# A three-branch decoder layer: the convolution's product turned token-major, the state space started eight weight pieces later, and vector and scalar work placed anew

## The chip, the cores and the metric

The kernel runs on one core of a Trainium2 chip. The metric is the time of one execution on the device in microseconds (us); before the change it is 1209.36 us, the median of three runs (1208.78 to 1209.36). The core has a matrix engine (TensorE, PE in the profile), a vector engine (VectorE, DVE), a scalar engine (ScalarE, ACT), GpSimd (POOL) and a queue for transfers (SyncE, SP). Each works through its own list of instructions in order and waits for the others by semaphores.

## The reference

One decoder layer on 256 tokens of width 2048, all in float32. One wide input projection feeds three branches; each branch is projected back to 2048 columns, weighted by a sigmoid gate and summed; an output projection, a residual and a norm follow.

```python
h = rms_norm(x, norm_w); proj = h @ w_in            # 18464 columns, split up
o_sb  = stick_breaking_attention(sb_q, sb_k, sb_v) * silu(sb_z)
xbc   = silu(causal_depthwise_conv(ssd_xbc, conv_w, conv_b))      # 4096 channels, 4 taps
x_ssm, b_in, c_in = split(xbc)
dt = softplus(ssd_dt + dt_bias);  a = -exp(a_log)
y  = ssd_chunked_scan(x_ssm heads, dt, a, b_in, c_in) + d_skip * x_ssm
o_ssd = gated_group_rms_norm(y, ssd_z, ssd_norm_w)
o_mem = memory_cross_attention(mem_q, rms_norm(mem), w_mem_kv) * silu(mem_z)
g_sb, g_ssd, g_mem = split(sigmoid(gate_pre + b_gate))
merged = g_sb*(o_sb @ w_branch_sb) + g_ssd*(o_ssd @ w_branch_ssd) + g_mem*(o_mem @ w_branch_mem)
out = rms_norm(x + merged @ w_out, final_norm_w)
```

In the scan a head's 256x256 matrix of decays is `exp(a_cum[l] - a_cum[s])` below the diagonal, times `cb[l,s]`; it multiplies `x * dt`.

## The kernel before

All large products stream their weights from memory in 408 **pieces** of 512 KB. A piece is loaded (`raw`, 4 buffers, L206), split by ScalarE into its upper half `wh` (L146) and by VectorE into the rest `wl = raw - wh` (L150), 3 buffers each, and used by TensorE in three matmuls per tile (upper by upper, upper by rest, rest by upper). So ScalarE and VectorE run ahead of TensorE by as much as three buffers allow: the split of a piece can begin when TensorE is done with the piece three earlier.

There are two forms of the product. `gemm` (L249) takes pieces of 256 rows by 512 columns, has the activations stationary and gives tokens in the partitions: 12 matmuls of 512 columns a piece. `gemm_cols` (L211), used by the convolution alone, takes 512 rows by 256 columns, has the weights stationary and gives channels in the partitions: for each of its 4 row tiles two matmuls of 512 columns (L229) and two of 256 (L233). Where `gemm`'s result is wanted with channels in the partitions, `turning` (L302) does it: two 32x32-block transposes on VectorE, one write to memory and four reads back from ScalarE's queue.

Order is set by hand. The pieces of all products form one sequence. After each piece `pump()` (L185) does two things: it runs what `defer(fn, n)` has put down for n pieces later, and it takes one step of one of two **lanes**, in turn. A lane is a queue of Python generators, and each `yield` ends a step. The attention heads (`sb_head`, L672) are in the lanes during the projections, the state space (`ssd_group`, L815, eight groups of four heads, worked in pairs) afterwards. So an instruction's place on its engine is fixed when the program is built, between the splits of two pieces.

In what follows **c1** is the first piece after the convolution's last, c2 the next, and so on. Pieces c1 to c8 are the first gate product, c9 to c12 the first branch product (`w_branch_mem`), c13 to c20 the next gate, and so on by twelve: four gates and four products of the memory branch, the same of the stick-breaking branch, then the state-space branch, whose products have eight pieces.

The steps of a state-space pair, in order: `cb` (two matmuls on TensorE, and the loads of the running decays `dec`, L823 to L828); `xs = x*dt`, a copy of `cb` to `cbs` and the causal mask (L830 to L846); the exponentials (`decay`, L849, four instructions of 128x128 for each of three tiles) and their product with `cbs` (`weigh`, L856); `y`, the products of both groups of the pair together (L869 to L883, 48 matmuls of 64x128); then skip, gate and norm (L887 to L916). The exponentials need ScalarE's table of exp and ln, the gates' sigmoid (`sigmoid`, L809) another; a change of table is an ACT_TABLE_LOAD of its own. `x` is turned for the products by `turn_x` (L758), once for two groups.

The convolution's four taps (`taps`, L745) are one multiply-add L747 and three L750 on VectorE for each of 32 tiles of 128 channels. `gate_evac` (L941) adds the bias on VectorE (L945) and takes the sigmoid on ScalarE; `branch_evac` (L949) multiplies by the gate (L954, L956) and sums the branches on GpSimd (L957).

Of the kernel before, what the change touches and what calls it, by code (L numbers as in the profile page):

```python
# [10 lines left out]
F32 = mybir.dt.float32  # L11
# [30 lines left out]
def trunk_kernel(  # L42
# [91 lines left out]
    nacx = const.tile([P, SSD_HEADS], F32, name="nacx")  # L134

# [371 lines left out]
    def dt_steps():  # L507
# [54 lines left out]
        nc.vector.tensor_tensor(nacx, nac[:, 0], ps[:, 2], ALU.subtract)  # L562
        yield
        pt = bank([SSD_HEADS, T], "act")
# [173 lines left out]
    def conv_evac(i0):  # L738
        def evac(acc):
            u = tmp.tile([P, 2, T], F32, tag="cu", name=nm("cu"), bufs=2)  # L740
            fold(u, acc)
            for b in range(2):
                defer(lambda b=b: taps(u[:, b], i0 + b), 1 + 2 * b)
# [9 lines left out]
        return evac  # L753

    x_rows = {}
    x_used = []

    def turn_x(m):  # L758

        src = cT[m // 2][:, 4 * (m % 2):4 * (m % 2) + 4]  # L760
        scratch = dram.tile([P, 4, T], F32, name=nm("scratch"))
        blocks = tmp.tile([P, 4, 2, 4, 32], F32, tag="blocks", name=nm("blocks"), bufs=1)
        rows = tmp.tile([P, 4, 2, 4, 32], F32, tag="turned", name=nm("turned"), bufs=1)

        def block(k):
            nc.vector.transpose(blocks[:, :, :, k].rearrange("p j t c -> p t j c"),
                                src[:, k].rearrange("p (t j c) -> p t j c", t=2, c=32))
# [41 lines left out]
    def sigmoid(a):  # L809
        nc.scalar.activation(a, a, AF.Sigmoid)  # L810
        tables[0] = False

    tables = [False]

    def ssd_group(g):  # L815

        heads = range(4 * g, 4 * g + 4)
        xT = [cT[i // 8][:, i % 8] for i in (2 * g, 2 * g + 1)]
# [4 lines left out]
        for j in range(2):  # L823
            nc.sync.dma_start(dec[j], acT[j, h0:h0 + 4].partition_broadcast(P))
# [298 lines left out]
```

## Time and profile before

| | |
|---|---|
| median of three runs | 1209.36 us |
| the profiled execution's own time | 1209.97 us |
| its span, first to last instruction | 1208.2 us |
| TensorE busy | 1197.4 us (99%) |
| VectorE busy | 792.0 us (66%) |
| ScalarE busy | 633.6 us (52%) |
| GpSimd busy | 51.5 us (4%) |
| granted TensorE clock | 0.999 |

The profile is one execution, taken by the hardware profiler. Its page gives each engine's busy time, the chain of work that ended last, and groups of instructions by line; the trace behind it answers for any stretch: a timeline row is start, duration, engine, line, operation, output<-input, count, and in brackets the time that the engine sat idle before it and what ended that. The ends of matmuls are modelled and overlap the next ones, so TensorE's pace is read from the starts. On ScalarE and VectorE too the next instruction may start a little before the one ahead of it ends.

### The profile page before, as it was taken

How to read it: one execution, taken by the hardware profiler on the slowest of the kernel's cores; microseconds unless marked ns; L12 is line 12 of the kernel's file. 1: busy time of each engine (PE TensorE's matmuls, PEld its weight loads, DVE VectorE, ACT ScalarE, POOL GpSimd, SP SyncE). 2: the span in 40 equal slices, each digit the busy share in tenths (PEclk: the TensorE clock that was granted, in tenths of full speed). 3: DMA queues.
4: the chain of work that ended last, by engine and by line, in shares of the span. 5: the costliest groups of instructions: out<-in, count | busy, mean ns of one | idle time of the engine just before them, and what ended most of it. 6: DMA issues, size and time to landing. Idle time of an engine off the chain costs nothing.

```text
span 1208.2 us, 15619 instructions
## 1 busy us (share of the span) xinstructions
PE 1197.4 (99%) x5812; PEld 1004.6 (83%) x5812; DVE 792.0 (66%) x1037; ACT 633.6 (52%) x842; POOL 51.5 (4%) x50
## 2 busy tenths in 40 slices
PE   8999999999999999999999999999999999999997
PEld 7888888888888888888888888888888888888886
DVE  5676664545555555888887858677677755555662
ACT  6754443364454444545665756485757534444551
POOL 0000000000000000010100000000000010110002
PEclk9999999999999999999999999999999999999999
DMA  9978687877775777665668676667756677778962
GB/s 315 363 225 237 205 251 234 251 234 214 205 210 171 216 220 228 190 186 167 187 176 258 212 223 216 214 206 218 223 181 201 209 216 220 227 220 280 295 205 88
DMA packets 170893, 265.72 MB, mean 220 GB/s; under 512 B 12032, under 2 KB 68032, under 8 KB 170688
## 3 DMA queue, kind: packets, MB, share of 16 engines
q1 hardware_dynamic: 134304, 227.41, 61.6%
q10 hardware_dynamic: 36512, 37.31, 9.5%
q8 instruction: 45, 0.74, 0.3%
q14 instruction: 32, 0.26, 0.1%
HBM read 249.97 MB, written 14.71 MB: 219 GB/s over the span
## 4 chain that ended last, share of the span: by engine, by line
PE 97%; issue 1%; DMA 1%; DVE 0%; ACT 0%; SPq 0%; POOLq 0%; POOL 0%; DVEq 0%; ACTq 0%
PE acc L269 25%; PE acc L270 25%; PE acc L271 25%; PE acc L229 10%; PE acc L233 5%; PE acc L458 1%; PE acc L459 1%; PE acc L457 1%; PE y L876 1%; DMA raw<-in_w_mem_kv_dram 1%; PE dtp L519 0%; PE acc L1077 0%; PE acc L1076 0%; PE acc L1075 0%; PE spo L710 0%
## 5 line engine op out<-in xcount | busy, mean ns | idle before, releaser
L150 DVE TENSOR_TENSOR wl<-raw,wh 128x1024 fp32r<-128x1024 f32 (+1 forms) x409 | 504.2, 1235 | 319.3 <-ACT wh L146 315.0
L146 ACT ACTIVATE wh<-raw 128x1024 fp32r<-128x1024 f32 (+1 forms) x409 | 431.5, 1056 | 434.9 <-PE acc L271 340.7
L269 PE MATMUL acc<-wh,hT 128*128 128x512 f32 x896 | 350.9, 392 | 0.0
L271 PE MATMUL acc<-wh,hT 128*128 128x512 f32 x896 | 348.8, 389 | 0.0
L270 PE MATMUL acc<-wl,hT 128*128 128x512 f32 x896 | 348.8, 389 | 0.0
L271 PEld LDWEIGHTS acc<-wh,hT 128*128 128x128 f32 x896 | 168.2, 188 | 35.5
L269 PEld LDWEIGHTS acc<-wh,hT 128*128 128x128 f32 x896 | 168.3, 188 | 34.1 <-issue 0.3
L270 PEld LDWEIGHTS acc<-wl,hT 128*128 128x128 f32 x896 | 168.3, 188 | 33.4
L229 PE MATMUL acc<-hT,wh 128*128 128x512 f32 x512 | 161.6, 397 | 0.0
L233 PEld LDWEIGHTS acc<-hT,wl 128*128 128x128 f32 x512 | 96.2, 188 | 22.7
L233 PE MATMUL acc<-hT,wl 128*128 128x256 f32 x512 | 100.7, 278 | 0.0
L229 PEld LDWEIGHTS acc<-hT,wh 128*128 128x128 f32 x512 | 78.1, 189 | 0.1
L269 PE MATMUL acc<-wh,oD 128*128 128x512 f32 x128 | 49.8, 389 | 0.0
L270 PE MATMUL acc<-wl,oD 128*128 128x512 f32 x128 | 49.8, 389 | 0.0
L271 PE MATMUL acc<-wh,oD 128*128 128x512 f32 x128 | 49.8, 389 | 0.0
L750 DVE SCALAR_TENSOR_TENSOR cT<-cu,wcols,cT 128x255 f32<-128x255 f32 (+2 forms) x96 | 46.4, 483 | 3.4
L957 POOL TENSOR_TENSOR merged<-merged,sig 128x512 f32<-128x512 f32 x16 | 25.8, 1637 | 512.3 <-DVE sig L956 512.3
L269 PE MATMUL acc<-wh,mT 128*128 128x512 f32 x96 | 37.3, 389 | 0.0
L270 PE MATMUL acc<-wl,mT 128*128 128x512 f32 x96 | 37.3, 389 | 0.0
L271 PE MATMUL acc<-wh,mT 128*128 128x512 f32 x96 | 37.3, 389 | 0.0
L270 PEld LDWEIGHTS acc<-wl,oD 128*128 128x128 f32 x128 | 24.0, 188 | 5.0
L271 PEld LDWEIGHTS acc<-wh,oD 128*128 128x128 f32 x128 | 24.0, 188 | 5.0
(239 smaller groups left out, 1283.6 us busy)
## 6 DMA issues: line engine op xcount, KB each, us to landing
raw<-in_w_in_dram SPq DMA_DIRECT2D x288, 512.0 KB, 4.3
raw<-in_w_branch_ssd_dram SPq DMA_DIRECT2D x32, 512.0 KB, 4.5
raw<-in_w_mem_kv_dram SPq DMA_DIRECT2D x31, 512.0 KB, 6.4
scratch<-blocks ACTq DMA_DIRECT2D x24, 512.0 KB, 4.3
raw<-in_w_out_dram SPq DMA_DIRECT2D x24, 512.0 KB, 6.1
turned<-scratch ACTq DMA_DIRECT2D x64, 128.0 KB, 4.6
raw<-in_w_branch_mem_dram SPq DMA_DIRECT2D x16, 512.0 KB, 4.8
raw<-in_w_branch_sb_dram SPq DMA_DIRECT2D x16, 512.0 KB, 5.0
```

The source lines that it names most:

```text
L146: nc.scalar.activation(hi, src, AF.Copy, **({} if scale is None else {"scale": scale}))
L150: nc.vector.tensor_tensor(lo, src, h32, ALU.subtract)
L229: nc.tensor.matmul(halves[b], wh[:, kt - k0, b * P:(b + 1) * P], lhs.both(kt), start=first, stop=False, skip_group_check=True)
L233: nc.tensor.matmul(halves[b][:, 1], wl[:, kt - k0, b * P:(b + 1) * P], lhs.at(kt)[0], start=False, stop=last, skip_group_check=True)
L269: nc.tensor.matmul(a, lh[:, tt], wh[:, j], start=first, stop=False)
L270: nc.tensor.matmul(a, lh[:, tt], wl[:, j], start=False, stop=False)
L271: nc.tensor.matmul(a, ll[:, tt], wh[:, j], start=False, stop=last)
L457: nc.tensor.matmul(a, lh[:, tt], wh[:, g], start=first, stop=False)
L458: nc.tensor.matmul(a, lh[:, tt], wl[:, g], start=False, stop=False)
L459: nc.tensor.matmul(a, ll[:, tt], wh[:, g], start=False, stop=last)
L750: nc.vector.scalar_tensor_tensor(a[:, s:T], u[:, 0:T - s], convw[:, 3 - s, i:i + 1], a[:, s:T], ALU.mult, ALU.add)
L957: nc.gpsimd.tensor_tensor(merged[t][:, cs], merged[t][:, cs], sig[:, t], ALU.add)
```

## The change

1. The convolution's product uses `gemm` and `turning` in place of `gemm_cols`. Out of the turned tile ScalarE copies two 128x512 tiles, and the first tap becomes a ScalarE activation with scale and bias.
2. The state space starts at c12, not c4: its `cb` matmuls stand after c12 and c13, not c4 and c5. For the state-space branch two gates are computed ahead of its first product, not one, so `finish()` is eight pieces later too.
3. `xs` loses its factor dt; the exponentials take `ln dt` in their bias instead (`shift`, from a new Ln in `dt_steps`), and `xs` is a plain copy on ScalarE, two pieces ahead of `y`'s step. A third load fills `dec[2]`.
4. The exponentials stand in three steps of four instructions, not two of six, and the first four in the same step as the copy `cbs`. A group's step moves on only when `x_rows` is there.
5. SiLU of two groups of x (the third and the fourth 512 channels) is done late, at the first two gates' sigmoids that follow: two sigmoids of 128x512 on ScalarE, each followed by a product on VectorE (`silu_late`); the buffer `sl` is single.
6. `gate_evac` adds its two halves in two pieces; `branch_evac` spreads its products, and the sum of the branches is on VectorE.

```diff
@@ dt_steps
+        nc.vector.tensor_scalar(z, dts, 1e-37, None, ALU.max)
+        nc.scalar.activation(z, z, AF.Ln)
+        yield
+        nc.vector.tensor_tensor(shift[:, 0:3:2], nac, z, ALU.add)
+        nc.vector.tensor_tensor(shift[:, 1], nacx, z[:, 0], ALU.add)
@@ convolution
+    def conv(i0):
+        when = (1, 3, 11, 13) if i0 == 12 else (1, 3, 5, 7)
+        def use(cols):
+            for k in (0, 2):
+                u = tmp.tile([P, 2, T], F32, tag="cu", name=nm("cu"), bufs=2)
+                nc.scalar.activation(blocked(u), tiles(cols, k, 2), AF.Copy)
+                for b in range(2):
+                    defer(lambda u=u, i=k + b: taps(u[:, i % 2], i0 + i), when[k + b])
...
         def taps(u, i):
             a = cT[i // 8][:, i % 8]
-            nc.vector.tensor_scalar(a, u, convw[:, 3, i:i + 1], convb[:, i:i + 1], ALU.mult,
-                                    ALU.add)
+            nc.scalar.activation(a, u, AF.Identity, scale=convw[:, 3, i:i + 1],
+                                 bias=convb[:, i:i + 1])
...
+        return turning(use)
+    def silu_late():
+        g = waiting.pop(0)
+        for k in range(4 * (g % 2), 4 * (g % 2) + 4, 2):
+            a = cT[g // 2][:, k:k + 2]
+            r = tmp.tile([P, 2, T], F32, tag="sl", name=nm("sl"), bufs=1)
+            nc.scalar.activation(r, a, AF.Sigmoid)
+            nc.vector.tensor_tensor(a, a, r, ALU.mult)
+        silu_done.add(g)
+    def squash(a):
+        nc.scalar.activation(a, a, AF.Sigmoid)
+        if waiting:
+            silu_late()
+        tables[0] = False
-        for j in range(2):
-            gemm_cols(hT, NKT, w_in, C_XBC + g * GW + 2 * j * P, conv_evac(4 * g + 2 * j))
+        gemm(hT, NKT, w_in, C_XBC + g * GW, conv(4 * g))
@@ ssd_group
-        decay(1)
-        decay(0, 0, 2)
-        yield
-        decay(0, 2, 4)
-        decay(2)
-        weigh(1)
-        yield
-        weigh(0)
-        weigh(2)
+        nc.scalar.activation(cbs, cb, AF.Copy)
+        decay(1)
+        for j in (0, 2):
+            nc.vector.tensor_tensor(dec[j], dec[j], over(cmask), ALU.add)
+        yield
+        decay(0)
+        weigh(1)
+        yield
+        decay(2)
+        weigh(0)
+        yield
+        while g // 2 not in x_rows:
+            yield
+        weigh(2)
...
-    defer(start_ssd, 4)
+    defer(lambda: turn_when(0), 7)
+    defer(start_ssd, 12)
@@ gates and branches
         def evac(acc):
-            for t in (1, 0):
-                nc.vector.tensor_tensor(sig[:, t], acc[t], sig[:, 0], ALU.add)
-            defer(lambda: sigmoid(sig), 1)
+            part(acc, 1)
+            defer(lambda: part(acc, 0), 1)
+            defer(lambda: squash(sig), 2)
...
-                    nc.gpsimd.tensor_tensor(merged[t][:, cs], merged[t][:, cs], sig[:, t],
-                                            ALU.add)
+        def add(t):
+            nc.vector.tensor_tensor(merged[t][:, cs], merged[t][:, cs], sig[:, t], ALU.add)
...
+            for gate in ((0, 1), (), (2,), (3,))[g] if br == 2 else (g,):
```

Three places show how it moves instructions. A row is line, operation, output<-input and size; the rows stand as their engine takes them, and each `wh` or `wl` row is the split of one piece.

VectorE, where the first pair's `dec` tiles get their mask. Before (`xs` is x*dt, `turned` the turned x):

```order
L150 TENSOR_TENSOR wl_5704<-raw_5701,wh_5703 128x1024
L835 TENSOR_TENSOR xs_5719<-turned_5255,dts 128x128 x4
L846 TENSOR_TENSOR dec_5665<-dec_5665,cmask 128x512
L846 TENSOR_TENSOR dec_5667<-dec_5666,cmask 128x512
L150 TENSOR_TENSOR wl_5734<-raw_5731,wh_5733 128x1024
```

Now, between the splits of c15 and c16 (`cT` with `cu` are the convolution's taps of its last group):

```order
L151 TENSOR_TENSOR wl_5639<-raw_5636,wh_5638 128x1024
L762 SCALAR_TENSOR_TENSOR cT_3782<-cu_5623,wcols,cT_3782 128x255
L762 SCALAR_TENSOR_TENSOR cT_3782<-cu_5623,wcols,cT_3782 128x254
L762 SCALAR_TENSOR_TENSOR cT_3782<-cu_5623,wcols,cT_3782 128x253
L996 TENSOR_TENSOR merged_5289<-acc_5471,sig_5291 128x512
L996 TENSOR_TENSOR merged_5290<-acc_5471,sig_5291 128x512
L887 TENSOR_TENSOR dec_5596<-dec_5596,cmask 128x512
L887 TENSOR_TENSOR dec_5598<-dec_5598,cmask 128x512
L151 TENSOR_TENSOR wl_5673<-raw_5670,wh_5672 128x1024
```

The x*dt products are gone; three taps and the first branch's two products now stand with the two masks between two splits.

VectorE, behind the products `y` of a pair. Before, the second pair (the first group's skip and gate, L889 and L892, then a split, the branch's products and the second group's):

```order
L889 SCALAR_TENSOR_TENSOR cT_3776<-cT_3776,wcols,y_6450 128x256 x2
L892 TENSOR_TENSOR zT_3072<-zT_3072,cT_3776 128x2x8x32
L150 TENSOR_TENSOR wl_6523<-raw_6520,wh_6522 128x1024
L954 TENSOR_TENSOR merged_5545<-acc_6361,sig_6143 128x512
L954 TENSOR_TENSOR merged_5546<-acc_6361,sig_6143 128x512
L889 SCALAR_TENSOR_TENSOR cT_3776<-cT_3776,wcols,y_6473 128x256 x2
L892 TENSOR_TENSOR zT_3072<-zT_3072,cT_3776 128x2x8x32
L150 TENSOR_TENSOR wl_6547<-raw_6544,wh_6546 128x1024
```

Now, the first pair, from `y` to the split of c26 (`sl` are the late SiLU's sigmoids, `blocks` a transpose of `turn_x`):

```order
L927 SCALAR_TENSOR_TENSOR cT_3781<-cT_3781,wcols,y_5835 128x256 x2
L930 TENSOR_TENSOR zT_3077<-zT_3077,cT_3781 128x2x8x32
L151 TENSOR_TENSOR wl_5910<-raw_5907,wh_5909 128x1024
L762 SCALAR_TENSOR_TENSOR cT_3782<-cu_5625,wcols,cT_3782 128x255
L762 SCALAR_TENSOR_TENSOR cT_3782<-cu_5625,wcols,cT_3782 128x254
L762 SCALAR_TENSOR_TENSOR cT_3782<-cu_5625,wcols,cT_3782 128x253
L833 STREAM_TRANSPOSE blocks_5815<-cT_3781 128x2x4x32
L786 TENSOR_TENSOR cT_3782<-cT_3782,sl_5931 128x512
L786 TENSOR_TENSOR cT_3782<-cT_3782,sl_5934 128x512
L927 SCALAR_TENSOR_TENSOR cT_3781<-cT_3781,wcols,y_5856 128x256 x2
L930 TENSOR_TENSOR zT_3077<-zT_3077,cT_3781 128x2x8x32
L151 TENSOR_TENSOR wl_5943<-raw_5940,wh_5942 128x1024
```

Between the same two splits there are now three taps, a transpose and two products that need ScalarE's sigmoids.

ScalarE, at the exponentials of the second pair. Before, the third pair's, whose rows have the same form as the second's but with a table load:

```order
L843 ACTIVATE cbs_6802<-cb_6744 128x384
L146 ACTIVATE wh_6808<-raw_6806 128x1024
L843 ACTIVATE cbs_6834<-cb_6776 128x384
L146 ACTIVATE wh_6840<-raw_6838 128x1024
L806 ACT_TABLE_LOAD
L853 ACTIVATE dec_6740<-dec_6740,nacx 128x128 x4
L853 ACTIVATE dec_6739<-dec_6739,nac 128x128 x2
L146 ACTIVATE wh_6866<-raw_6864 128x1024
L853 ACTIVATE dec_6772<-dec_6772,nacx 128x128 x4
L853 ACTIVATE dec_6771<-dec_6771,nac 128x128 x2
L146 ACTIVATE wh_6891<-raw_6889 128x1024
```

Now, the second pair, between the splits of c36 and c38:

```order
L884 ACTIVATE cbs_6202<-cb_6149 128x384
L878 ACTIVATE dec_6144<-dec_6144,shift 128x128 x4
L981 DMA sig_6210<-in_b_gate_dram 128x512
L147 ACTIVATE wh_6215<-raw_6213 128x1024
L810 ACT_TABLE_LOAD
L810 ACTIVATE sig_5904<-sig_5904 128x1024
L785 ACTIVATE sl_6232<-cT_3782 128x512
L785 ACTIVATE sl_6235<-cT_3782 128x512
L884 ACTIVATE cbs_6238<-cb_6180 128x384
L806 ACT_TABLE_LOAD
L878 ACTIVATE dec_6175<-dec_6175,shift 128x128 x4
L147 ACTIVATE wh_6249<-raw_6247 128x1024
```

A gate's sigmoid, the late SiLU's two, two table loads, a copy of `cb` and four exponentials now stand between the splits of c37 and c38. In the third pair the same place (between the splits of c61 and c62) has the table load, the gate's sigmoid, the second table load and four exponentials. Table loads in the whole program: 21 before, 25 now.

More of the change, by code (lines that the diff above doesn't have):

```diff
@@ L752, in taps, with conv_done, exp_ln, turn_when @@
                                                ALU.mult, ALU.add)
-        return evac
+        return turning(use)
+    silu_done = set()
+    tables = [False]
+    def conv_done(g):
+        if g > 1:
+            waiting.append(g)
+            return
+        a = cT[g // 2][:, 4 * (g % 2):4 * (g % 2) + 4]
+        nc.scalar.activation(a, a, AF.Silu)
+        silu_done.add(g)
[6 more added lines that the diff above has]
+            nc.vector.tensor_tensor(a, a, r, ALU.mult)
+        silu_done.add(g)
+    waiting = [zT[i // 2][:, 4 * (i % 2):4 * (i % 2) + 4] for i in range(4)]
+    for i, g in enumerate((4, 5, 6, 7, 0, 1, 2, 3)):
+        gemm(hT, NKT, w_in, C_XBC + g * GW, conv(4 * g))
+        if g >= 4:
+            waiting.append(cT[g // 2][:, 4 * (g % 2):4 * (g % 2) + 4])
+        else:
+            for j in range(min(3, len(waiting))):
+                silu(waiting.pop(0), 1 + j)
+    oD = []
+    ssd_done = []
+    pair = []
+    def exp_ln():
+        if not tables[0]:
+            nc.scalar.preload_act_table_set("natural_log_exp_and_others")
+            tables[0] = True
+    def squash(a):
[3 more added lines that the diff above has]
+        tables[0] = False
+    def turn_when(m):
+        if m in silu_done:
+            turn_x(m)
+        else:
+            defer(lambda: turn_when(m), 1)
     x_rows = {}
@@ L762, in turn_x @@
         blocks = tmp.tile([P, 4, 2, 4, 32], F32, tag="blocks", name=nm("blocks"), bufs=1)
-        rows = tmp.tile([P, 4, 2, 4, 32], F32, tag="turned", name=nm("turned"), bufs=1)
+        rows = []
         def block(k):
@@ L822, in ssd_group @@
         h0 = heads[0]
-        for j in range(2):
-            nc.sync.dma_start(dec[j], acT[j, h0:h0 + 4].partition_broadcast(P))
+        for j in range(3):
+            nc.sync.dma_start(dec[j], acT[(j + 1) // 2, h0:h0 + 4].partition_broadcast(P))
         cb = bank([P, 3, P], "cb")
@@ L829, in ssd_group, with decay, weigh @@
         yield
+        cbs = small2([P, 3, P], "cbs")
+        over = lambda a: a.unsqueeze(1).to_broadcast([P, 4, P])
+        def decay(j):
+            exp_ln()
+            for e in range(4):
+                nc.scalar.activation(dec[j][:, e], dec[j][:, e], AF.Exp,
+                                     bias=shift[:, j, h0 + e:h0 + e + 1])
+        def weigh(j):
+            nc.vector.tensor_tensor(dec[j], dec[j], over(cbs[:, j]), ALU.mult)
+        nc.scalar.activation(cbs, cb, AF.Copy)
+        decay(1)
@@ L839, in ssd_group @@
         x_used.append(g)
         if len(x_used) % 2 == 0 and len(x_used) < SSD_GROUPS:
-            turn_x(len(x_used) // 2)
-        cbs = small2([P, 3, P], "cbs")
-        nc.scalar.activation(cbs, cb, AF.Copy)
-        over = lambda a: a.unsqueeze(1).to_broadcast([P, 4, P])
-        for j in (0, 2):
-            nc.vector.tensor_tensor(dec[j], dec[j // 2], over(cmask), ALU.add)
-        yield
-        def decay(j, e0=0, e1=4):
-            a = (nac[:, 0], nacx, nac[:, 1])[j]
-            exp_ln()
-            for e in range(e0, e1):
-                nc.scalar.activation(dec[j][:, e], dec[j][:, e], AF.Exp,
-                                     bias=a[:, h0 + e:h0 + e + 1])
@@ L856, in weigh @@
-        def weigh(j):
-            nc.vector.tensor_tensor(dec[j], dec[j], over(cbs[:, j]), ALU.mult)
-        decay(1)
-        decay(0, 0, 2)
-        yield
-        decay(0, 2, 4)
-        decay(2)
-        weigh(1)
-        yield
-        weigh(0)
-        weigh(2)
+            turn_when(len(x_used) // 2)
         yield
```

77 lines of the change are left out of this document (34 added, 43 removed).

## The prediction

> **What bounds the kernel now.** I read the page first, then the waits, then timelines of TensorE, ScalarE and VectorE. The page says that TensorE does nearly everything on the chain that ended last:
>
> ```profile
> PE 1197.4 (99%) x5812; PEld 1004.6 (83%) x5812; DVE 792.0 (66%) x1037; ACT 633.6 (52%) x842; POOL 51.5 (4%) x50
> ...
> PE 97%; issue 1%; DMA 1%; DVE 0%; ACT 0%; SPq 0%; POOLq 0%; POOL 0%; DVEq 0%; ACTq 0%
> ```
>
> The waits (us in total, times, longest) say who waits for whom:
>
> ```profile
> ACT wh L146 <- PE acc L271: 340.7, 223, 3.1
> ...
> DVE wl L150 <- ACT wh L146: 315.0, 270, 5.6
> ...
> ACT wh L146 <- DMA raw<-in_w_mem_kv_dram: 5.2, 6, 2.0
> ...
> PEld acc L458 <- DVE wl L150: 0.9, 2, 0.7
> ```
>
> ScalarE waits for TensorE to free a `wh` buffer, VectorE waits for ScalarE, splits wait little for weights (the third row, weights of the program's start), and the last row is the longest of TensorE's waits for a `wl`: 0.9 us in the whole run. So work on the vector engines costs nothing until it eats the lead that three buffers give, and TensorE's own pace costs everywhere. Both matter here. The pace first, from TensorE's timeline in the convolution and in a product of the form `gemm`:
>
> ```profile
> 577.01 0.62 PE L229 MATMUL acc<-hT,wh 128*128 128x512 f32 x2
> 577.47 0.40 PE L233 MATMUL acc<-hT,wl 128*128 128x256 f32 x2
> ...
> 579.10 0.63 PE L229 MATMUL acc<-hT,wh 128*128 128x512 f32 x2
> ```
> ```profile
> 439.82 0.39 PE L269 MATMUL acc<-wh,hT 128*128 128x512 f32 x1
> ...
> 442.54 0.39 PE L269 MATMUL acc<-wh,hT 128*128 128x512 f32 x1
> ```
>
> Start to start, two 512s and two 256s take 0.697 us (three steps: 579.10-577.01 = 2.09); twelve 512s take 2.72 us, 0.227 each.
>
> The lead is read where the engines run freely, TensorE's first matmul of a piece and ScalarE's next split:
>
> ```profile
> 697.72 0.39 PE L269 MATMUL acc<-wh,hT 128*128 128x512 f32 x1
> ...
> 697.92 1.06 ACT L146 ACTIVATE wh<-raw 128x1024 fp32r<-128x1024 f32 x1 [1.66 <-PE acc L271]
> ```
>
> ScalarE's split begins 0.2 us after TensorE ended the piece three earlier, takes 1.06, VectorE's takes 1.22 (row at 768.36 below); TensorE wants `wl` with a piece's second matmul, two pieces later. That leaves 5.44+0.23-0.2-1.06-1.22 = 3.2 us. More backlog than this stops TensorE.
>
> **The convolution's product.** 256 row steps at 0.697 are 178.4 us; the 768 matmuls that replace them, 64 pieces of twelve at 2.72, take 174.1. **Gain 4.3 us**, all on TensorE's path. The columns streamed are the same (2x512+2x256 a step, 256 steps, against 768x512); only the pace of the narrow ones goes. The transposes, 16 on VectorE and 16 copies on ScalarE, replace 16 sums L247 and 16 copies L246, and the first tap leaves VectorE: there the load of the stretch falls. The turning's writes and reads are those that the other products of this form already make beside a TensorE that doesn't wait; if they were late, ScalarE's copies would hold its splits (last rival).
>
> **Prices for the rest.** ScalarE at the first pair's exponentials, and later a sigmoid:
>
> ```profile
> 673.41 0.49 ACT L843 ACTIVATE cbs<-cb 128x384 f32<-128x384 f32 x1 [1.96 <-PE cb L828]
> 673.80 1.05 ACT L146 ACTIVATE wh<-raw 128x1024 fp32r<-128x1024 f32 x1
> 674.87 1.28 ACT L806 ACT_TABLE_LOAD   x1
> 676.17 1.28 ACT L853 ACTIVATE dec<-dec,nacx 128x128 f32<-128x128 f32 x4
> 677.35 0.68 ACT L853 ACTIVATE dec<-dec,nac 128x128 f32<-128x128 f32 x2
> 677.94 1.04 ACT L146 ACTIVATE wh<-raw 128x1024 fp32r<-128x1024 f32 x1
> 678.89 1.26 ACT L853 ACTIVATE dec<-dec,nacx 128x128 f32<-128x128 f32 x4
> ...
> 688.41 1.06 ACT L810 ACTIVATE sig<-sig 128x1024 f32<-128x1024 f32 x1
> 689.38 1.99 ACT L146 ACTIVATE wh<-raw 128x1024 fp32r<-128x1024 f32 x2
> ```
>
> To the next start: a split 0.95, a table load 1.30, four exponentials 1.18, `cbs` 0.39, a gate's sigmoid 0.97. `cbs` starts 0.28 after TensorE's first matmul behind `cb`:
>
> ```profile
> 672.56 0.59 PE L827 MATMUL cb<-cT,cT 128*128 128x256 f32 x2
> ...
> 673.13 0.47 PE L269 MATMUL acc<-wh,hT 128*128 128x512 f32 x1
> 673.45 0.39 PE L270 MATMUL acc<-wl,hT 128*128 128x512 f32 x1
> ```
>
> So a piece with `cb` behind it lasts 2.72+0.57, the next one 0.09 more. VectorE at the second pair's `y`, with TensorE, and at the taps:
>
> ```profile
> 765.26 2.84 PE L876 MATMUL y<-dec,xs 128*64 128x128 f32 x48
> 768.03 0.50 PE L269 MATMUL acc<-wh,hT 128*128 128x512 f32 x1
> ...
> 773.83 0.39 PE L270 MATMUL acc<-wl,hT 128*128 128x512 f32 x1
> ```
> ```profile
> 628.51 1.52 DVE L750 SCALAR_TENSOR_TENSOR cT<-cu,wcols,cT 128x255 f32<-128x255 f32 x3
> 629.95 1.22 DVE L150 TENSOR_TENSOR wl<-raw,wh 128x1024 fp32r<-128x1024 f32 x1
> ...
> 766.84 0.87 DVE L889 SCALAR_TENSOR_TENSOR cT<-cT,wcols,y 128x256 f32<-128x256 f32 x2 [4.55 <-PE y L876]
> ...
> 768.36 1.22 DVE L150 TENSOR_TENSOR wl<-raw,wh 128x1024 fp32r<-128x1024 f32 x1
> 769.49 1.28 DVE L954 TENSOR_TENSOR merged<-acc,sig 128x512 f32<-128x512 f32 x2
> 770.69 0.86 DVE L889 SCALAR_TENSOR_TENSOR cT<-cT,wcols,y 128x256 f32<-128x256 f32 x2
> ...
> 772.20 1.22 DVE L150 TENSOR_TENSOR wl<-raw,wh 128x1024 fp32r<-128x1024 f32 x1
> ```
>
> Skip and gate of a group 1.52, a split 1.13, two products of 512 1.20 (0.60 each; the mask is the same size), three taps 1.44. This stretch tests the method: `wl` ended at 773.42 and TensorE wanted it at 773.83, 0.41 to spare, no stop. Not shown in the trace of before are the copies from the turned tile, the sigmoids of 512 and the tap on ScalarE; their nearest rows:
>
> ```profile
> L246 ACT ACTIVATE cu<-acc 128x512 f32<-128x512 f32 x16 | 9.6, 598 | 27.6 <-PE acc L233 27.6
> ...
> L894 ACT ACTIVATE xs<-zT 128x512 f32<-128x512 f32 x8 | 5.0, 625 | 6.4 <-DVE zT L892 6.3
> ...
> L146 ACT ACTIVATE oD<-zT,wcols 128x256 fp32r<-128x256 f32 x16 | 7.1, 493 | 0.0
> L766 DVE STREAM_TRANSPOSE blocks<-cT 128x256 f32<-128x256 f32 x16 | 7.0, 438 | 0.0
> L957 POOL TENSOR_TENSOR merged<-merged,sig 128x512 f32<-128x512 f32 x16 | 25.8, 1637 | 512.3 <-DVE sig L956 512.3
> ```
>
> Less about 0.1 of overlap with the next, as for the split: copy 0.50, sigmoid 0.53 (its end 0.63 after its start), scaled tap 0.39, transpose 0.36. Bounds for each are 0.1 below and the full row above.
>
> **Four places where the lead doesn't suffice.** Times count from TensorE's end of the piece named.
>
> *c16, VectorE* (from the end of c11). TensorE starts c12 at 0, c13 at 3.29, c14 at 6.67, c15 at 9.48, c16 at 12.20, wanting `wl` at 12.43. ScalarE splits c13 at -2.5; tap, table, sigmoid, split of c14 end by 2.06; two copies 3.06; `cbs` can't start before 3.57, to 3.96; table and four exponentials 6.44; split of c15 ends 7.50. VectorE: split 8.67, taps 10.11, two products 11.31, two masks 12.51, split of c16 ends 13.73. **1.3 us late.**
>
> *c26, VectorE* (from its first row behind `y`, which stood at 766.84 for before). TensorE wants c26's `wl` at 773.83-766.84 = 6.99. Skip and gate 1.52, split 2.65, taps 4.09, transpose 4.45, first late-SiLU product ends 5.14; only then may ScalarE's second sigmoid refill the single buffer, ending 5.83; second product 6.50, second group 8.02, split ends 9.24. **2.25 late.** Behind that instruction are queued the splits of c26 and c27 on both engines.
>
> *c38, ScalarE* (from the end of c33). TensorE wants `wl` at 12.43 as above. `cbs` waits for `cb` till 3.57; exponentials to 5.14; split of c37 6.09; table 7.39; sigmoid 8.36; late sigmoid ends 8.99; product on VectorE 9.74; second sigmoid 10.33; `cbs` 10.72; table, after the copy's end, 12.1; exponentials 13.3; split ends 14.34, VectorE's 15.59. **3.15 late.**
>
> *c62, ScalarE* (from the end of c55). Wanted at 17.87. `cbs` and exponentials of the two groups, held by both `cb`s, end 8.52; splits and one more step bring c61's split to 11.60; table, sigmoid, table, exponentials 16.45; split ends 17.51, VectorE's 18.76. **0.9 late.** In the fourth pair the same four stand two pieces further from `cb`, and 0.2 is left over.
>
> Sum 7.6, net 7.6-4.3 = **+3.3 us**. On the profiled execution's 1209.97 that is 1213.3; it stands 0.61 above the median, so the median goes from 1209.36 to 1212.7.
>
> **At nothing.** The branches' sum on VectorE (16 at 0.60 where GpSimd took 1.64) and the spread gate halves lie, by these prices and the order, in pieces with at most some 4 us of vector work between lighter ones: a backlog under 2 us, covered by the lead of 3.2. Uncovered, the sums alone would cost 16x0.6 = 9.6. The third `dec` load stands on SP's queue ahead of weight loads, and the third row of the waits says how little splits wait for those; bound 0 to 1 us. The Ln and its table load (1.30) lie in a stretch of light steps. `finish()` and the state space both move eight pieces, so that distance stays.
>
> [...] The row at 674.87 gives 1.30 us for a change of table, from the split's end to the first exponential. [...]
>
> **Rivals.**
> *Even* (28 in 100): the backlog is smaller, by 0.9 to 5.6 us over the four places, as when ScalarE's instructions overlap more than my rows show. The places then sum to 2.0 to 6.7: net -2.3 to +2.4, 1207.1 to 1211.8. For it: every place is a difference of two sums of about 10 us.
> *Faster* (7): TensorE's pace is won, and the lead never runs out but at c38. The point is a sum of stalls under 1.9 us; with c38 at 1.5 alone, 1209.36-4.3+1.5 = 1206.6. It needs c37's list of 8.2 us on ScalarE to shrink by 1.7. Against it: those instructions stand in one engine's order, at prices read from rows. This also is the case that the spreading does what its words say.
> [...]
> *Late transfers* (5): ScalarE's copies from the turned tile or the `dec` tiles wait for memory, holding splits; one microsecond for each of the eight turned groups on top, 1220.7.
>
> The forecast has 58. A median within 0.2% (2.4 us) of before is about what a measurement of this kernel can't tell from no change. Slower by more than that: the forecast nearly whole, the two dear rivals: 0.64. Same 0.29, faster 0.07. The range is 1208.0 to 1216.5: 1.2 us off each place on one side (7.6-4.7-4.3 = -1.4), and on the other the full rows, some ten instructions of 0.1 more at each place (7.6+3.8-4.3 = +7.1).
>
> **What would show it.** Right: the convolution's matmuls at 0.227 and that stretch about 4.3 us shorter; TensorE waiting for `wl` or `wh` in four spots, c16, c26, c38, c62, of 1 to 3 us, nowhere else over 0.5; GpSimd off the branches. Wrong: no `wl` waits at c26 and c38 (the lead is larger than counted); the convolution's pace unchanged; waits of ScalarE for transfers.

## The result, and the profile after

| | before | after |
|---|---|---|
| median | 1209.34 us (1208.78 to 1209.36) | 1221.85 us (1219.03 to 1223.13) |
| the profiled execution's own time | 1209.97 us | 1221.24 us |
| its span | 1208.2 us | 1219.2 us |
| granted TensorE clock | 0.999 | 0.996 |

The changed kernel is slower by 12.5 us: the ratio is 1.010, with a 95% interval of 1.0089 to 1.0112. The prediction had +3.3 us. Its side was right, its size was not. The four executions of the changed kernel also lie 4 us apart, those of the one before 0.6; more on that below.

The page of the changed kernel first, engines and chain:

```profile
PE 1199.2 (98%) x5556; PEld 994.5 (82%) x5556; DVE 775.3 (64%) x996; ACT 661.4 (54%) x897; POOL 24.0 (2%) x34
...
PE 92%; ACT 2%; DVE 2%; DMA 2%; issue 1%; SPq 0%; POOLq 0%; POOL 0%; DVEq 0%; ACTq 0%
```

TensorE's share of the chain falls from 97 to 92%; ScalarE, VectorE and transfers have 2% each. The waits (us in total, times, longest) say who stops it. In the kernel before, TensorE's largest wait for a `wl` held 0.9 us in the whole run:

```profile
PEld acc L271 <- DVE wl L151: 9.4, 8, 2.4
...
ACT sl L785 <- DVE cT L786: 5.6, 2, 4.9
ACT wh L147 <- DMA raw<-in_w_in_dram: 5.4, 2, 3.1
```

The second row is the single `sl` buffer (4.9 us of it at c26); the third is new: splits that wait for weights, one of the prediction's own signs of being wrong. (Line numbers are one higher than before's at the splits and matmuls.)

**The convolution's pace** came as predicted. TensorE's first matmul of the convolution and of c1, after:

```profile
469.07 0.39 PE L270 MATMUL acc<-wh,hT 128*128 128x512 f32 x1
...
653.67 0.39 PE L270 MATMUL acc<-wh,hT 128*128 128x512 f32 x1
```

and before:

```profile
469.74 0.62 PE L229 MATMUL acc<-hT,wh 128*128 128x512 f32 x2
...
658.25 0.40 PE L269 MATMUL acc<-wh,hT 128*128 128x512 f32 x1
```

That is 184.6 us against 188.5: 3.9 gained, 4.3 predicted.

**What was lost behind c1** is read from TensorE's starts, first `wl` matmul to first `wl` matmul: a quiet piece takes 2.72 us (more with `cb` or `y` behind it), and what is over that is the stop.

| place | predicted | measured |
|---|---|---|
| c14, c15, c16 | 1.3 (c16 alone) | 0.6 + 2.2 + 2.2 = 5.0 |
| c26 | 2.25 | 2.2 |
| the two pieces behind c26 | 0 | 1.4 + 0.4 = 1.8 |
| c38 | 3.15 | 3.2 |
| the piece behind c38 | 0 | 1.5 |
| c62 | 0.9 | 1.2 |
| c17, c86, c102 | 0 | 0.1 + 0.2 + 0.4 |
| sum | 7.6 | 15.6 |

Less the convolution's 3.9, and less 0.7 because it also began that much earlier (469.07 against 469.74), 15.6 leaves 11.0, which is what the two spans differ by (1219.2 less 1208.2). The executions that were profiled differ by 11.3, the medians by 12.5. (The one before was 0.6 above its median, the one after 0.6 below.) So c26, c38 and c62 came out as worked out, and two things were missed: nearly 4 us at c14 to c16, and 3.3 us in pieces *behind* two of the stops.

VectorE's list at c26, from its first row behind `y` to the split that TensorE waits for, has the second late sigmoid's wait in the middle:

```profile
724.41 0.87 DVE L927 SCALAR_TENSOR_TENSOR cT<-cT,wcols,y 128x256 f32<-128x256 f32 x2 [3.66 <-PE y L914]
...
728.86 0.65 DVE L786 TENSOR_TENSOR cT<-cT,sl 128x512 f32<-128x512 f32 x1
730.21 0.69 DVE L786 TENSOR_TENSOR cT<-cT,sl 128x512 f32<-128x512 f32 x1 [0.70 <-ACT sl L785]
...
732.33 1.22 DVE L151 TENSOR_TENSOR wl<-raw,wh 128x1024 fp32r<-128x1024 f32 x1
```

and ScalarE's at c38, between the splits of c37 and c38, the change of table:

```profile
762.59 1.05 ACT L147 ACTIVATE wh<-raw 128x1024 fp32r<-128x1024 f32 x1
...
768.30 1.28 ACT L806 ACT_TABLE_LOAD   x1
769.60 1.27 ACT L878 ACTIVATE dec<-dec,shift 128x128 f32<-128x128 f32 x4
770.78 1.04 ACT L147 ACTIVATE wh<-raw 128x1024 fp32r<-128x1024 f32 x1
```

These are the lists of the prediction. Now what lies behind the stops. TensorE's timeline at c26:

```profile
731.18 0.49 PE L270 MATMUL acc<-wh,hT 128*128 128x512 f32 x1
733.61 0.50 PE L271 MATMUL acc<-wl,hT 128*128 128x512 f32 x1 [1.93 <-DVE wl L151]
...
735.61 0.63 PE L272 MATMUL acc<-wh,hT 128*128 128x512 f32 x1
736.04 0.63 PE L270 MATMUL acc<-wh,hT 128*128 128x512 f32 x1
...
738.53 0.40 PE L270 MATMUL acc<-wh,hT 128*128 128x512 f32 x1
738.76 0.40 PE L271 MATMUL acc<-wl,hT 128*128 128x512 f32 x1
```

Nothing is waited for after 733.61, and yet from 735.2 to 738.2 a matmul takes 0.43 us from start to start instead of 0.23. The busy time by window shows why (window, its length, TensorE busy and its matmuls, granted clock, transfers' share, GB/s):

```profile
731.61:735.02 3.41, 1.48 (x7) 1.00 0.18 32
735.02:738.43 3.41, 3.41 (x10) 0.50 0.81 259
738.43:741.85 3.42, 3.42 (x16) 1.00 0.67 196
769.16:772.57 3.41, 1.20 (x5) 1.00 0.00 0
772.57:775.98 3.41, 2.85 (x7) 0.50 0.47 133
```

The granted clock is one half for exactly 3.41 us, once behind c26 and once behind c38, and 37.55 us lie between the two starts: eleven times 3.413.

At c14, ScalarE's timeline:

```profile
682.12 0.36 ACTq L981 DMA_DIRECT2D sig<-in_b_gate_dram  x1
682.59 1.06 ACT L147 ACTIVATE wh<-raw 128x1024 fp32r<-128x1024 f32 x1 [3.18 <-DVE sig L983]
...
684.16 1.28 ACT L810 ACT_TABLE_LOAD   x1
685.45 1.06 ACT L810 ACTIVATE sig<-sig 128x1024 f32<-128x1024 f32 x1
688.79 1.06 ACT L147 ACTIVATE wh<-raw 128x1024 fp32r<-128x1024 f32 x1 [2.28 <-DMA raw<-in_w_in_dram]
```

The prediction had the split of c13 begin at 681.1 (2.5 us ahead of TensorE's c12, which began at 683.6): it began 1.5 us later. It had that of c14 end at 685.7: it waited for its weights and ended at 689.9, 4.2 us later. The predicted list had 0.5 us of waiting for `cb` behind that split, which fell away; the rest ran at the predicted prices, 3.7 us late, and that is the excess at c14 to c16 (5.0 - 1.3). The weights were issued here, on SP's queue:

```profile
673.36 0.38 SPq L208 DMA_DIRECT2D raw<-in_w_in_dram  x1
673.83 3.58 SPq L866 DMA_DIRECT2D dec<-acT  x3
678.71 7.78 SPq L208 DMA_DIRECT2D raw<-in_w_in_dram  x4
```

They were issued at 678.7 and had landed at 688.7, ten microseconds later, behind the pair's `dec` loads. Median times from issue to landing between 664 and 690 us (KB each, us last):

```profile
raw<-in_w_in_dram SPq DMA_DIRECT2D x5, 512.0 KB, 9.2
raw<-in_w_branch_mem_dram SPq DMA_DIRECT2D x3, 512.0 KB, 5.7
dec<-acT SPq DMA_DIRECT2D x6, 256.0 KB, 8.8
...
scratch<-blocks ACTq DMA_DIRECT2D x1, 512.0 KB, 9.0
```

### The profile page after: what moved, and what is told of

It is laid out like the page before. It is cut to its first block, busy times and chain, and to the rows that moved or that the text cites. A ratio compares the mean times of both kernels' runs of the same rounds, so it can differ in the third digit from the quotient of the medians.

```text
span 1219.2 us, 15178 instructions
## 1 busy us (share of the span) xinstructions
PE 1199.2 (98%) x5556; PEld 994.5 (82%) x5556; DVE 775.3 (64%) x996; ACT 661.4 (54%) x897; POOL 24.0 (2%) x34
## 4 chain that ended last, share of the span: by engine, by line
PE 92%; ACT 2%; DVE 2%; DMA 2%; issue 1%; SPq 0%; POOLq 0%; POOL 0%; DVEq 0%; ACTq 0%
PE acc L271 28%; PE acc L270 28%; PE acc L272 28%; PE acc L459 1%; PE acc L460 1%; PE acc L458 1%; DVE wl L151 1%; PE y L914 1%; ACT wh L147 1%; DMA turned<-scratch 1%; DMA raw<-in_w_mem_kv_dram 1%; DMA raw<-in_w_in_dram 1%; ACT dec L878 0%; ACT L806 0%; PE dtp L520 0%
## 5 line engine op out<-in xcount | busy, mean ns | idle before, releaser
L271 PE MATMUL acc<-wl,hT 128*128 128x512 f32 x1152 | 450.7, 391 | 6.6 <-DVE wl L151 6.6
L270 PE MATMUL acc<-wh,hT 128*128 128x512 f32 x1152 | 452.9, 393 | 2.9 <-ACT wh L147 2.9
L272 PE MATMUL acc<-wh,hT 128*128 128x512 f32 x1152 | 449.8, 390 | 0.0
L271 PEld LDWEIGHTS acc<-wl,hT 128*128 128x128 f32 x1152 | 217.1, 188 | 52.4 <-DVE wl L151 9.4
L270 PEld LDWEIGHTS acc<-wh,hT 128*128 128x128 f32 x1152 | 217.0, 188 | 48.2 <-ACT wh L147 4.2
L272 PEld LDWEIGHTS acc<-wh,hT 128*128 128x128 f32 x1152 | 217.0, 188 | 45.6
L310 DVE STREAM_TRANSPOSE blocks<-acc 128x512 f32<-128x512 f32 x48 | 31.4, 691 | 0.0
L878 ACT ACTIVATE dec<-dec,shift 128x128 f32<-128x128 f32 x96 | 30.5, 390 | 0.0
L270 PEld LDWEIGHTS acc<-wh,oD 128*128 128x128 f32 x128 | 24.0, 188 | 5.0
L272 PEld LDWEIGHTS acc<-wh,oD 128*128 128x128 f32 x128 | 24.0, 188 | 5.0
L458 PE MATMUL acc<-wh,memT 128*128 128x512 f32 x64 | 25.2, 393 | 1.7 <-ACT memT L147 1.7
L459 PE MATMUL acc<-wl,memT 128*128 128x512 f32 x64 | 25.1, 393 | 0.4 <-DVE wl L151 0.4
```

Source lines behind the costliest of these rows:

```text
L270: nc.tensor.matmul(a, lh[:, tt], wh[:, j], start=first, stop=False)
L271: nc.tensor.matmul(a, lh[:, tt], wl[:, j], start=False, stop=False)
L272: nc.tensor.matmul(a, ll[:, tt], wh[:, j], start=False, stop=last)
L310: nc.vector.transpose(blocks[:, t].rearrange("p j k c -> p k j c"), rows[t].rearrange("p (k j c) -> p k j c", k=4, j=4))
L458: nc.tensor.matmul(a, lh[:, tt], wh[:, g], start=first, stop=False)
L459: nc.tensor.matmul(a, lh[:, tt], wl[:, g], start=False, stop=False)
```

## The experiments

Two theories came out of this. **Transfers**: at c14 a burst of loads for the state space, the third `dec` load among them, holds the weights up. **Clock**: a stop that leaves TensorE idle for much of a 3.4 us window is followed by a window at half clock, as behind the 1.93 us idle before 735.02 and the 2.21 us before 772.57 above; that costs another 1.5 to 1.8 us, by the table. Their rivals are the prediction's own view (the third load costs nothing, the engine lists alone are late) and a cause of the slow matmuls other than the stop. The expectations name stops loosely; the places are those of the table above. Medians of the kernel before beside these runs were 1209.22 to 1209.26 us.

### Late SiLUs moved

```diff
     def squash(a):
         nc.scalar.activation(a, a, AF.Sigmoid)
-        if waiting:
-            silu_late()
+        squashed.append(a)
+        if len(squashed) == 2:
+            defer(silu_late, 4)
+        elif len(squashed) == 4:
+            silu_late()
```

> The changed kernel with the two late SiLUs moved: the first four pieces behind c26's sigmoid, while ScalarE still holds the sigmoid table, the second to the sigmoid of c50, where no exponentials stand. Clock theory: the stop at c26 falls from 2.2 us to about 0.2, that at c38 from 3.2 to about 1.2, and as neither then leaves TensorE idle for most of a 3.4 us window, the two stretches at half the granted clock (1.6 and 1.5 us lost) go too: 4.0 and 3.1, 1214.7. Rival, the slow matmuls behind the two stops have another cause (backlog of the weights, the load of memory): they stay, 1217.9. Second rival, the two lists are not what stops TensorE: no change, 1221.9.

Measured: 1217.47 us (1216.84 to 1220.03), ratio 1.0073 (1.0061 to 1.0086). At c26 the stop fell by 2.0 us and the slow pieces behind it went (1.3 and 0.4 less): 3.7 of the expected 4.0. At c38 the stop fell by 0.3 only, from 3.2 to 2.9. The waits of ScalarE between 745 and 762 us tell why:

```profile
ACT wh L147 <- DMA raw<-in_w_branch_mem_dram: 5.9, 2, 4.5
```

A split of a piece ahead of c38 waits 4.5 us for weights issued behind the second pair's `dec` loads. With one list shortened, the transfers became what was late. This profile, the slowest of the five executions (granted clock 0.995, 0.996 in the others), also lost more than the changed kernel's in two places: behind c38 the clock was at half for two windows (3.0 us lost, 1.5 before), and c62's stop was 2.0 us instead of 1.0, behind a split that waited 5.8 us for weights. So the median lies nearer to the rival's number, but for a reason that neither theory had; the clock theory's part is seen at c26, where nothing but the stop was changed.

### The gate's load issued by GpSimd

```diff
-        nc.scalar.dma_start(sig[:, 0], b_gate[c0:c0 + GW].partition_broadcast(P))
+        nc.gpsimd.dma_start(sig[:, 0], b_gate[c0:c0 + GW].partition_broadcast(P))
```

> The changed kernel with the load of the gate's bias rows issued by GpSimd, which is idle, instead of ScalarE. In the changed kernel ScalarE stands from 680.8 to 682.1 us at that issue before c14's list, and c13's split starts 1.5 us later than it could. If that wait is what makes c14's stop longer than predicted: 1.5 us less, 1220.4. Transfer theory: ScalarE then waits the longer for the weights of c14, which land at 688.7 either way; no change, 1221.9 within 0.6.

Measured: 1221.63 us (1217.63 to 1224.63), ratio 1.0089 (1.0075 to 1.0103). The median is the changed kernel's. ScalarE's stand at that issue isn't what makes c14 late. With the issue gone, c13's split waits for its own weights instead:

```profile
684.23 1.06 ACT L147 ACTIVATE wh<-raw 128x1024 fp32r<-128x1024 f32 x1 [3.82 <-DMA raw<-in_w_in_dram]
```

In the changed kernel these weights were issued at 673.36 and landed at 682.04, 0.5 us before the split began, so the stand could cost little there either. The stops at c14 to c16 sum to 4.6 us, 0.4 less than in the changed kernel. The five executions span 7 us, and the granted clock goes with them: 0.997 at 1217.63, 0.992 at 1224.63.

### Stops made on purpose

The kernel before, with idle copies on ScalarE (128x512, `ident` into a tile that nobody reads) at fourteen pieces where the profile shows a full lead:

```diff
         now[0] += 1
+        if now[0] in stops:
+            for _ in range(stops[now[0]]):
+                nc.scalar.activation(idle.rearrange("p (a b) -> p a b", b=P),
+                                     ident.unsqueeze(1).to_broadcast([P, 4, P]), AF.Copy)
```

> The kernel before with 8 to 14 idle copies of 128x512 on ScalarE (0.50 us each) at fourteen quiet pieces, so that TensorE stops there for about 0.8 to 3.8 us (copies less the lead of 3.2 us). Clock theory: behind every stop over some 2.5 us the granted clock is 0.5 for one stretch of 3.4 us, which costs 1.7 us more; behind those under 1.5 us never; between, it depends on where the stop falls against windows of 3.4 us that run freely. Rival: the half clock of the changed kernel comes from something else near c26 and c38, and no made stop is followed by one.

Measured in one execution: 1257.64 us, granted clock 0.987. A stop is counted here as the time that TensorE is idle. There are eight stretches of 3.41 us at half clock ahead of the program's end, each behind one made stop. Three of the places by window, a stop of 1.9 us that falls into one window, one of 1.9 us that falls across two, and the longest:

```profile
169.11:172.52 3.41, 1.55 (x6) 1.00 0.60 154
172.52:175.93 3.41, 3.41 (x10) 0.50 0.88 273
984.89:988.30 3.41, 2.26 (x9) 1.00 0.13 38
988.30:991.71 3.41, 3.41 (x17) 1.00 0.81 252
...
1128.25:1131.66 3.41, 3.41 (x9) 0.50 0.56 168
```

The five stops of 1.2 us and less were never followed by half clock. Of nine from 1.9 us up, eight were; the ninth is the third row above, where the window kept 2.26 us of work. The clock theory stands: it isn't the place, it is the idle time, and how it falls against the windows.

### One `dec` load less

```diff
-        for j in range(3):
+        for j in range(2):
             nc.sync.dma_start(dec[j], acT[(j + 1) // 2, h0:h0 + 4].partition_broadcast(P))
...
-        for j in (0, 2):
-            nc.vector.tensor_tensor(dec[j], dec[j], over(cmask), ALU.add)
+        for j in (2, 0):
+            nc.vector.tensor_tensor(dec[j], dec[0], over(cmask), ALU.add)
...
-                                     bias=shift[:, j, h0 + e:h0 + e + 1])
+                                     bias=shift[:, j % 2, h0 + e:h0 + e + 1])
```

> The changed kernel with two loads of decay rows a group instead of three; the third tile takes its mask sum and its shift from the first tile's, so the output is not the reference's. Every other instruction stays. Transfer theory: near c14 ScalarE's split waits 2.3 us for weights that were issued at 678.7 us and landed 10 us later, behind loads of decay rows of 256 KB; one load less for each of two groups lets them land 1 to 2 us earlier, TensorE's stops at c14 to c17 fall from 5.0 to 3 or 4 us, nothing changes elsewhere, and the time is 1219.8 to 1220.9. Rival, the third load costs nothing (as the prediction has it): the weights land as late, and the time stays at 1221.9 within 0.6.

Measured: 1216.04 us (1215.02 to 1219.22), ratio 1.0063 (1.0051 to 1.0076). That is 5.8 us less than the changed kernel, where the transfer theory had 1 to 2. In the profile c14 and c15 don't stop at all, and c16 stops for 1.5 us, close to the prediction's own number (1.3): 3.5 us of stop were due to this load. The rest goes with the clock: granted 0.999 in the median execution, 0.992 to 0.997 in the four of the changed kernel. The stops at c26 (2.2), c38 (3.2) and c62 (1.0) are all still there, but in this execution no window behind them is at half clock, because here the one at c26, like that at c38, falls across two:

```profile
725.44:728.85 3.41, 2.80 (x12) 1.00 0.70 270
728.85:732.26 3.41, 2.10 (x9) 1.00 0.28 71
732.26:735.68 3.42, 3.42 (x17) 1.00 0.82 257
```

With nothing but the engine lists left, the four places sum to 1.5 + 2.2 + 3.2 + 1.0 = 7.9 us, against 7.6 in the prediction.

### The three loads spread

All three loads are kept, but issued one a piece ahead of the pair:

```diff
+    def load_dec(g, j):
+        d = (tb if j == 2 else ta)([P, 4, P], "dec")
+        nc.sync.dma_start(d, acT[(j + 1) // 2, 4 * g:4 * g + 4].partition_broadcast(P))
+        decs.setdefault(g, {})[j] = d
+    def load_pair(g, wait):
+        if g < SSD_GROUPS:
+            for n in range(6):
+                defer(lambda n=n: load_dec(g + n % 2, (1, 0, 2)[n // 2]), wait + n)
...
     defer(start_ssd, 12)
+    load_pair(0, 5)
```

> The changed kernel with all three loads kept, but issued one a piece in the six pieces ahead of a pair's first product instead of three at once. Transfer theory: the weights of c14 are no longer behind a burst of 1.5 MB, ScalarE's wait of 2.3 us for them goes, and the stops at c14 to c17 fall from 5.0 to between 1.3 (the engine lists as predicted) and 2.8 us; those at c26 and c38 stay, with half clock behind them: 1218.2 to 1219.7. Rival, what fills the transfers is the turning's traffic and not these loads: 1221.9 within 0.6.

Measured: 1217.74 us (1214.92 to 1218.97), ratio 1.0070 (1.0057 to 1.0082): faster than the changed kernel by 4.1. Of c14 to c16 only c16 stops, for 1.4 us. The same group of transfers as above, from 664 to 690 us:

```profile
raw<-in_w_in_dram SPq DMA_DIRECT2D x6, 512.0 KB, 4.7
raw<-in_w_branch_mem_dram SPq DMA_DIRECT2D x3, 512.0 KB, 5.6
...
scratch<-blocks ACTq DMA_DIRECT2D x1, 512.0 KB, 4.1
```

Weights land in 4.7 us, not 9.2, and ScalarE waits for none between 676 and 705 us. So the same six loads, 1.5 MB, cost no stop when they are issued one a piece. They are also issued earlier for it, all before 665 us and not from 670.6 to 676.9; which of the two does it, this run doesn't separate.

### A third load in the kernel before

```diff
-        for j in range(2):
-            nc.sync.dma_start(dec[j], acT[j, h0:h0 + 4].partition_broadcast(P))
+        for j in range(3):
+            nc.sync.dma_start(dec[j], acT[(j + 1) // 2, h0:h0 + 4].partition_broadcast(P))
...
-            nc.vector.tensor_tensor(dec[j], dec[j // 2], over(cmask), ALU.add)
+            nc.vector.tensor_tensor(dec[j], dec[j], over(cmask), ALU.add)
```

> The kernel before with one edit: three loads of decay rows a group, the third tile no longer made from the second by the mask sum. If a burst of three loads for each of two groups is too much for the transfers beside the weights wherever it stands: waits of ScalarE for weights of 1 to 4 us near c4 and c26, and 1210.5 to 1214. Rival, it takes the turning's traffic of the convolution and of the first x rows beside it, as at c14 in the changed kernel: 1209.2 within 0.5.

Measured: 1209.44 us (1208.95 to 1211.11), ratio 1.0005 (0.9996 to 1.0014). In the kernel before, the third load is free, as the prediction had said of it: TensorE doesn't stop once. So its price belongs to the changed kernel, where it stands in another place. What is there beside it is the convolution's late turning, the write and reads of the first x rows, and a gate's rows; which of these weighs most was not taken apart.

### Both moved, then the groups four pieces later

The spread loads and the moved SiLUs together:

> The spread loads and the late SiLUs moved, together. Without the latter alone 1217.5. Transfer theory: c14 to c17 lose 2.2 to 3.7 us of their stop; in the kernel with late SiLUs moved, ScalarE waited 4.5 us at c36 for weights behind the second pair's loads, which goes too, so that c38's stop comes down from 2.9 to the 1.2 of the engine lists; no stop is left that takes TensorE out for two thirds of a window of 3.4 us, so the half clock goes but for an odd window: 1210.5 to 1213. Rival, the lists and not the transfers are what is late at c14 and c38: 1216 to 1217.5.

Measured: 1211.38 us (1211.12 to 1213.76), ratio 1.0021 (1.0012 to 1.0030). c16 stops for 1.4 us, c38 for 1.3 (expected 1.2), c62 for 1.0; no window between c1 and the program's end is at half clock (granted clock 0.999). With `start_ssd` at 16, `turn_when(0)` at 11 and the first loads four pieces later as well:

> As the kernel with spread loads and late SiLUs moved, and the state space's groups start another four pieces later, so that the sigmoids of c14 and c38 stand ahead of a pair's exponentials and not between them, with one change of table less at each. List theory: the stops at c16 and c38 (1.3 and 1.2 us) go, that at c62 stays at about 1, the convolution's 3.7 us are kept: 1206.5 to 1208, faster than the kernel before. Rival, the stop moves with the groups (to c86, or to c27 where the first pair's skip and gate now stand): 1209 to 1211.

Measured: 1209.84 us (1209.76 to 1210.34), ratio 1.0005 (0.9996 to 1.0014). The stops at c16 and c62 went. Others came, as the rival had it: 0.8 at c30, where the second late sigmoid waits behind skip and gate, 1.6 at c38, where the sigmoid now stands between two normalizations with two changes of table, and 1.3 at c86.

### The sigmoid a piece later

```diff
-            defer(lambda: squash(sig), 2)
+            defer(lambda: squash(sig), 3)
...
-            defer(silu_late, 4)
+            defer(silu_late, 1)
```

> The kernel with spread loads, late SiLUs moved and the groups four pieces later, with the gate's sigmoid one piece later (behind both of a pair's normalizations at c38, not between them, with two changes of table less) and the first late SiLU at c28, behind a skip-and-gate group less. List theory: of the stops that are left, c29's 0.8 and c37's 1.6 us go, c85's 1.3 stays: 1207.4 within 0.6, faster than the kernel before by 1 to 2.5 us. Rival, the sigmoid only moves into another list (c62, where it now stands behind the wait for the second product and ahead of four exponentials): 1209 to 1210.

Measured: 1207.84 us (1207.46 to 1208.70), ratio 0.9987 (0.9978 to 0.9996): faster than the kernel before, by 1.4 us of the 3.9 that the convolution gives. c30 and c38 no longer stop; one stop is left (its row in the expectation is c85, it stands at c87), of 1.6 us.

### The branches' sum back on GpSimd

The same kernel, with the sum as it was in the kernel before:

```diff
         def add(t):
-            nc.vector.tensor_tensor(merged[t][:, cs], merged[t][:, cs], sig[:, t], ALU.add)
+            nc.gpsimd.tensor_tensor(merged[t][:, cs], merged[t][:, cs], sig[:, t], ALU.add)
```

> The same kernel with the branches' sum back on GpSimd. As the prediction has it the sum on VectorE costs nothing, being covered by the lead: the time is that of the kernel beside it within 0.4. Rival, it lengthens VectorE's lists where the lead is used up: faster than that by 0.6 to 2.

Measured: 1210.51 us (1210.18 to 1210.78), ratio 1.0009 (1.0000 to 1.0018). It is 2.7 us *slower* than with the sum on VectorE, which neither theory had. VectorE at c63 to c65:

```profile
831.62 1.23 DVE L151 TENSOR_TENSOR wl<-raw,wh 128x1024 fp32r<-128x1024 f32 x1 [1.97 <-ACT wh L147]
...
833.36 2.38 DVE L901 TENSOR_TENSOR dec<-dec,cmask 128x512 f32<-128x512 f32 x2
835.67 1.21 DVE L151 TENSOR_TENSOR wl<-raw,wh 128x1024 fp32r<-128x1024 f32 x1
...
838.00 2.31 DVE L151 TENSOR_TENSOR wl<-raw,wh 128x1024 fp32r<-128x1024 f32 x1
```

and GpSimd in the same stretch:

```profile
833.58 1.62 POOL L1027 TENSOR_TENSOR merged<-merged,sig 128x512 f32<-128x512 f32 x1 [254.28 <-DVE sig L1014]
837.56 1.68 POOL L1027 TENSOR_TENSOR merged<-merged,sig 128x512 f32<-128x512 f32 x1 [2.36 <-DVE sig L1014]
```

While GpSimd adds, a split on VectorE takes 2.31 us, not 1.21, and two mask sums take 2.38 us, not 1.28 (the changed kernel's at 835.28). So these two sums each hold VectorE up by 1.1 us, where the same sum on VectorE takes 0.6, and here this part of the change makes VectorE's lists *shorter*. TensorE stops for 0.5 and 0.7 us at c64 and c65, and for 0.7 and 0.7 at c88 and c89: 2.6 of the 2.7 us.

## Why the prediction was right or wrong

Two steps failed: a load that it put at nothing, and a stop that it took for its own length. By the spans of the profiled executions the change cost 11.0 us where the prediction had 3.3. Of the 7.7 us between them, 3.7 are the excess at c14 to c16 and 3.3 the half clock; the other 0.7 are small terms.

*The convolution's product*: right, 3.9 us against 4.3. The pace is 2.72 us a piece as worked out; what else stands in that stretch takes 0.4 more (184.6 - 64 x 2.72 = 10.5 us, before 188.5 - 178.4 = 10.1).

*The lead of 3.2 us, and the lists at c26, c38 and c62*: right. Stops of 2.2, 3.2 and 1.2 us against 2.25, 3.15 and 0.9, and VectorE's list at c26 ended 9.1 us after the first row behind `y` (724.41 to 733.55) against 9.24. The prices of one instruction each, read from the kernel before, were good enough for new lists of a dozen. c38 also bears out the row for a change of table: from the load at 768.30 to the exponential at 769.60 there are 1.30 us. One of the "two dear rivals" in the forecast's chances (2 in 100) supposed a dearer change of table; no run shows one, and these 1.30 us are what was measured.

*"The third `dec` load stands on SP's queue ahead of weight loads, and the third row of the waits says how little splits wait for those; bound 0 to 1 us"*: this step failed. It cost 3.5 us of stop at c14 to c16. The row it leans on told of the kernel before, where the load is indeed free (1.0005); but the change puts the burst in another place, and how weights land there can't be read from a trace in which it doesn't stand there. Why it is dear at this place stays open. Late transfers were a rival, at 5 in 100 and 1220.7 us; they came at one place, through the splits' weights, and not through ScalarE's copies at eight turned groups, so the nearness of that number is chance.

*The sum of the stops* (7.6): this step failed too, for a term was missing. The prediction took a stop for its own length. Two of them were followed by 3.41 us at half clock, which cost 3.3 us in the profiled execution; how many such stretches there are changes from one execution to the next (granted clock 0.992 to 0.997 in four). None of the rivals had this. The forecast's place list ("nowhere else over 0.5") was right for the waits but for c14 and c15.

*At nothing*, the rest: the branches' sum on VectorE did cost nothing, and its sign was missed: in the last experiment's kernel it frees 0.5 us at each of the two sums shown there (1.1 us less 0.6). The gate halves and `finish()` made no stop of their own that the profile shows; they weren't run alone. At c86, in the fourth pair, where 0.2 us was to be left over, 0.2 was lost; at c102, which the prediction doesn't name, 0.4.

## What to carry to other kernels

Where engines work ahead of a matmul by a few buffers, lists of instructions at measured prices gave the stops here to a few tenths of a microsecond (2.2, 3.2 and 1.2 us against 2.25, 3.15 and 0.9); the loads that move with them need the same care, and they are to be priced at the *new* place. A stop can cost twice its length (2.9 us at c38 and 3.0 behind it with the SiLUs moved), and behind the five made stops of 1.2 us and less the clock stayed full, so breaking a long stop into short ones should pay before anything is taken away (that alone was not run). A gain on the bounding engine (3.9 us here) is kept only if everything that moved with it is placed anew: the same change was worth +12.5 or -1.4 us by where six loads, two SiLUs, the groups and a sigmoid stood.

## What the runs showed of the hardware

**The half clock.** The changed kernel's two half-clock stretches last 3.41 us each and start 37.55 us apart; with the made stops, the starts at 172.52 and 1128.25 lie 955.73 us apart. These are 11 and 280 times 3.413 us, so windows can be counted off in such steps from the starts. In the traces of the kernel before and of the changed kernel, behind the warm-up matmuls, the windows at full clock with 1.93, 2.21 and, at the two programs' ends, 3.41 us of TensorE idle are followed by one at half; none with less is (the longest have 1.81, 1.76 and 1.55). With the made stops, of two windows shown above, the one with 1.86 us idle is followed by half clock, the one with 1.15 is not. So what stood behind a stop of some 2 us went by how it fell on the windows: c26's 2.2 us, which left 1.93 idle in one window of the changed kernel, left 0.61 and 1.31 in two with one `dec` load less, and the clock stayed full. The changed kernel's window at 772.57, itself at half clock and with 0.56 us idle, was followed by one at full clock. How the stops fall is the likely reason why the changed kernel's executions differ by 4 us (granted clock 0.997 at 1219.03, 0.992 at 1223.13). The kernel before has no such stops; its four executions differ by 0.6 us, 27 later ones by 2.3, all at 0.998 or 0.999.

**GpSimd beside VectorE.** With the sum on GpSimd, a split beside a sum of 1.68 us (128x512) takes 2.31 us, not 1.21, and two mask sums beside one of 1.62 us take 2.38, not 1.28. In the kernel before, where these sums are on GpSimd too, the split at 840.65 takes 2.31 us beside a pair of sums of 2.7 us, and those at 875.90, 986.48, 1030.00 and 1073.52 take 1.65 us, each beside a pair of 3.5 us.

**Transfers.** Between 664 and 690 us, beside the turning's traffic, 512 KB of `w_in` landed in 9.2 us (median) with six loads of 256 KB issued in one place, in 6.7 with four, and in 4.7 with the six issued one a piece ahead of it.
